# A hybrid recurrent decoder step on one core: compact diagonal blocks of inverses, and w_in read by groups of eight rows

## The chip, the cores and the metric

The kernel runs on one core of one Trainium2 chip, in float32. The metric is the device time of one launch in microseconds (us). TensorE, VectorE (DVE), ScalarE (ACT), GpSimd (POOL) and SyncE (SP) run side by side, each with its instructions in order; SP and ScalarE issue the DMAs, which 16 DMA engines carry out.

## The reference, cut to what matters

One layer: a normalised input is multiplied by w_in (1024 x 8208), and the columns of the product feed an RG-LRU branch, a gated-DeltaNet branch, their gates and two merge gates. In DeltaNet, each chunk of tokens needs the inverse of a unit lower-triangular matrix.

```python
u = rms_norm(x, norm_pre)
z = jnp.einsum('btd,de->bte', u, w_in)
...
decay = jnp.where(causal, jnp.exp(jnp.where(causal, diff, 0.0)), 0.0)
M = jnp.where(strict, jnp.einsum('nbhik,nbhjk->nbhij', kb, kc) * decay, 0.0)
P = -M
Tinv = jnp.broadcast_to(jnp.eye(C, dtype=M.dtype), M.shape)
for _ in range((C - 1).bit_length()):
    Tinv = Tinv + jnp.einsum('nbhij,nbhjk->nbhik', Tinv, P)
    P = jnp.einsum('nbhij,nbhjk->nbhik', P, P)
u = jnp.einsum('nbhij,nbhjv->nbhiv', Tinv, vc * bc[..., None])
...
merged = jax.nn.sigmoid(m_lru) * p_lru + jax.nn.sigmoid(m_gdn) * p_gdn
y = jnp.einsum('btd,de->bte', merged, w_out)
```

There are 2048 prompt tokens and 64 sample tokens, D_MODEL is 1024, and DeltaNet has 8 heads of 128 x 128.

## The kernel before, in words

The prompt is worked through in four blocks of 512 tokens (blkno 0 to 3); the 64 sample tokens ride along in block 0. x is loaded with tokens on the partitions, normalised (u_norm), transposed by TensorE in 32 (block 0: 40) pieces and split into a high and a low part (u_tile); each tile k of u holds 128 rows of the contraction. Every product with a weight is done three times (high x high, high x low, low x high: lines 551, 553, 555 in proj), in pieces of 128 output columns.

Weights. Their order is a list, worder. In block 0 each piece is loaded from its input (wload), split into two parts by ScalarE and VectorE (split, called in wfetch), and the pair whl is stored into a scratch tensor dW (wstore, line 279). Blocks 1 to 3 load whl from dW (line 300). whl has three buffers. In most of the first part of block 0 two pieces of w_in are loaded at once (raw, 256 columns, line 271), else one (raws, 128 columns, line 265); the loads put row k*128 + p of the weight on partition p, for k from 0 to 7.

DeltaNet runs in two phases per block. In the first, t_gram makes M for each head and chunk of 128 tokens and stores it in dM (line 780). When all 8 heads are done, t_inv loads the four 32 x 32 diagonal blocks of all 32 matrices as 128 small matrices, one per partition, and inverts them on VectorE (tri_inverse). The inverses and their transposes are stored into dD and dDT (lines 848 and 849), which hold full 128 x 128 matrices; their remaining parts have to be zero, and t_zero stores the zeros in block 0 (line 504). In the second phase, t_inv2 loads for each head M (Mt), the inverses (Dn) and their transposes (R) (lines 990 to 992), and a Neumann step on TensorE fills in the blocks of R off the diagonal; t_chain then runs over the chunks.

TensorE's order is fixed by a planner in the Python code, Weave: side tasks are generators that yield a time in ns or a condition, and proj lets it run one step of each due task after every product. The order of the other engines and of SP's queue is found by a scheduler at build time from the program order and its own estimates, so that it can change with any edit. A DMA on SP can also have to wait for the landing of an earlier one whose semaphore it takes over.

The lines that matter:

```python
SP.dma_start(raw, src[:, c:c + w].rearrange("(k p) c -> p k c", p=128))
...
tr(t[:, n:n + m], xt[:m, k * 128:(k + 1) * 128], ident[:m, :m])
...
SP.dma_start(dD[:, q, q], r[0][q])
SP.dma_start(dDT[:, q, q], r[1][q])
```

Of the kernel before, what the change touches and what calls it, by code (L numbers as in the profile page):

```python
# [154 lines left out]
def body(ctx, tc, x_prompt, x_sample, state_lru_conv, state_lru_h, state_gdn_conv, state_gdn_S,  # L155
# [28 lines left out]
    def gtile():  # L184
        t = pg.tile([128, 512], F32, name="g", tag="g")
        return t
# [8 lines left out]
    def tr(out, in_, idn):  # L195
        T.transpose(out, in_, idn)  # L196
        W.pe(TR)
# [41 lines left out]
    dW = [dram.tile([128, 2, 1024], F32, name=f"dW{i}") for i in range(len(wplace))]  # L239
    wstores, wraws = [], {}  # L240

    wready = []
    wlast = [None]
    wnext, lnext = [0], [0]
# [8 lines left out]
    def wload(n):  # L253

        src, c = e = worder[n]
        if key(e) in wraws:
            return
        if isinstance(c, tuple):
            raw = rw.tile([128, 4, 256], F32, name="rawo", tag="raws")
            SP.dma_start(raw, src[c[1] * 512:(c[1] + 1) * 512, c[0] * 256:(c[0] + 1) * 256]  # L260
                         .rearrange("(k p) c -> p k c", p=128))
            wraws[key(e)] = raw
        elif not (paired[0] <= n < paired[1] or paired[2] <= n < paired[3]):
            raw = rw.tile([128, 8, 128], F32, name="raws", tag="raws")
            SP.dma_start(raw, src[:, c:c + 128].rearrange("(k p) c -> p k c", p=128))
            wraws[key(e)] = raw
        else:
            two = [key(x) for x in worder[n:n + 7]].count((src.tensor.name, c + 128))
            w = 128 + 128 * two
            raw = rp[0].tile([128, 8, w], F32, name="raw", tag="raw")  # L270
            SP.dma_start(raw, src[:, c:c + w].rearrange("(k p) c -> p k c", p=128))
            for j in range(1 + two):
                wraws[src.tensor.name, c + 128 * j] = raw[:, :, 128 * j:128 * j + 128]

# [72 lines left out]
    def u_tile(xh, k):  # L347
        hi = pA.tile([128, TB + NS], F32R, name="a", tag="a")
        lo = pA.tile([128, TB + NS], F32R, name="a", tag="a")
        for gi, grp in enumerate([xh[:4]] + ([xh[4:]] if len(xh) > 4 else [])):  # L350
            t = gtile()
            n = 0
            for xt, m in grp:
                tr(t[:, n:n + m], xt[:m, k * 128:(k + 1) * 128], ident[:m, :m])
                n += m
            cs = slice(gi * 512, gi * 512 + n)
            act(hi[:, cs], t[:, :n], AF.Copy, scale=npre[:, k:k + 1])
            V.scalar_tensor_tensor(out=lo[:, cs], in0=t[:, :n], scalar=npre[:, k:k + 1],
                                   in1=hi[:, cs].bitcast(F32), op0=OP.mult, op1=OP.subtract)
        return hi, lo  # L360
# [23 lines left out]

    dk = dram.tile([H, 128, TB + NS], F32, name="dk")
    dM = dram.tile([H * NCH, 128, 128], F32, name="dM")
    dD = dram.tile([H * NCH, 128, 128], F32, name="dD")
    dDT = dram.tile([H * NCH, 128, 128], F32, name="dDT")
    dE = dram.tile([H, 128, TB], F32, name="dE")
    dtm = dram.tile([16, 128, TB + NS], F32, name="dtm")  # L390
    dgc = dram.tile([H * NCH, 128], F32, name="dgc")
# [19 lines left out]
    rows = lambda a: a.rearrange("o (g p) -> (o g) p", p=128)  # L411
    with tc.tile_pool(name="init", bufs=2, side="right") as ip:
        with tc.tile_pool(name="u0", bufs=1) as up:
            r0 = ip.tile([8, 128], F32, name="r0")
            SP.dma_start(r0, rows(norm_pre))
            xh = u_load(0, up)
            t = gtile()
            tr(t[:, :8], r0, ident[:8, :8])
            V.tensor_copy(npre, t[:, :8])
            wraw = ip.tile([128, 8, 16], F32, name="wraw", bufs=1)  # L420
            SP.dma_start(wraw, win[:, C_B:C_B + 16].rearrange("(k p) c -> p k c", p=128))
            u_norm(xh, up)
            for n in range(2):
                wload(n)
                lnext[0] += 1
            SP.dma_start(dtb, bass.AP(tensor=gdn_dt_bias.tensor, offset=gdn_dt_bias.offset, ap=[[0, 128], [1, 8]]))
            SP.dma_start(negA, bass.AP(tensor=gdn_A_log.tensor, offset=gdn_A_log.offset, ap=[[0, 128], [1, 8]]))
            u = [u_tile(xh, k) for k in range(8)]
            zz = ip.tile([128, 96], F32, name="zz", bufs=1)
            V.memset(zz, 0.0)  # L430
            V.tensor_copy(wst[:, 256:352], zz)
            V.tensor_copy(wst3[:, :, 0:16], wraw)
            V.tensor_tensor(out=wst3[:, :, 16:32], in0=wraw, in1=wst3[:, :, 0:16].bitcast(F32), op=OP.subtract)
            wfetch(2)
        G.affine_select(out=tri, in_=ones, pattern=[[1, 128]], compare_op=OP.is_ge, fill=0.0,
                        base=0, channel_multiplier=-1)
        G.affine_select(out=offm.rearrange("p (a b) -> p a b", b=32), in_=ones.rearrange("p (a b) -> p a b", b=32),
                        pattern=[[-32, 4], [0, 32]], compare_op=OP.is_ge, fill=0.0, base=-32,
                        channel_multiplier=1)
        V.tensor_scalar(offm, offm, -1.0, None, op0=OP.mult)  # L440

        blk = const.tile([64, 64], F32, name="blk")
        blk3 = blk.rearrange("p (a b) -> p a b", b=8)
        G.affine_select(out=blk3, in_=ones[:64, :64].rearrange("p (a b) -> p a b", b=8),
                        pattern=[[-8, 8], [0, 8]], compare_op=OP.is_ge, fill=0.0, base=0, channel_multiplier=1)
        G.affine_select(out=blk3, in_=blk3, pattern=[[8, 8], [0, 8]], compare_op=OP.is_ge, fill=0.0,
                        base=7, channel_multiplier=-1)
        tris = const.tile([64, 64], F32, name="tris")
        V.tensor_tensor(out=tris, in0=blk, in1=tri[:64, :64], op=OP.mult)
        negs = const.tile([64, 64], F32, name="negs")  # L450
        V.tensor_scalar(negs, tris, 1.0, BIG, op0=OP.subtract, op1=OP.mult)
        bsel = blk3[:, :, 0]
        G.memset(halog, 0.0)
        G.memset(halol, 0.0)
        G.memset(hlast, 0.0)
        tc.keep_in_program_order(A.activation(negA, negA, AF.Exp))
        V.tensor_scalar(negA, negA, -1.0, None, op0=OP.mult)
# [39 lines left out]
    def t_zero(pool):  # L497

        z = pool.tile([128, 4, 128], F32, name="lru7")
        G.memset(z, 0.0)  # L500
        for h in range(H):
            yield 7000.0
            for dst in (dD, dDT):
                SP.dma_start(dst[4 * h:4 * h + 4].rearrange("c i j -> i c j"), z)
        yield 7000.0
        SP.dma_start(dDs.rearrange("h i j -> i h j"),
                     z[:64].rearrange("p a b -> p (a b)").rearrange("p (a b) -> p a b", b=64))
        zeroed[0] = True
# [22 lines left out]
    for blkno in range(NBLK):  # L531
# [299 lines left out]
        def t_inv():  # L831
            yield lambda: all(kdone)
            Mb = kl.tile([128, 32, 32], F32, name="Mb", tag="Mbinv", bufs=1)
            for b in range(4):
                q = slice(32 * b, 32 * b + 32)
                SP.dma_start(Mb[q], dM[:, q, q])
            if sb:
                Mbs = kl.tile([64, 8, 8], F32, name="Mbs", tag="Mbinvs", bufs=1)
                for b in range(8):
                    q = slice(8 * b, 8 * b + 8)  # L840
                    SP.dma_start(Mbs[q], dMs[:, q, q])
            yield 3000.0
            r = []
            yield from tri_inverse(kl, 32, 128, Mb, "inv", r)
            yield lambda: zeroed[0]
            for b in range(4):
                q = slice(32 * b, 32 * b + 32)
                SP.dma_start(dD[:, q, q], r[0][q])
                SP.dma_start(dDT[:, q, q], r[1][q])
            yield T_IN  # L850
            invdone[0] = True
            if sb:
                r = []
                yield from tri_inverse(kl, 8, 64, Mbs, "invs", r)
                for b in range(8):
                    q = slice(8 * b, 8 * b + 8)
                    SP.dma_start(dDs[:, q, q], r[1][q])
# [121 lines left out]
        def h2t(nm, bufs=B2, shape=None):  # L979
            return h2.tile(shape or [128, NCH, 128], F32, name=nm, tag=nm, bufs=bufs)  # L980

        def t_inv2(h):

            d = st_[h]
            hc = slice(NCH * h, NCH * h + NCH)
            d["kT"] = h2t("kT", B2, [128, NB])
            SP.dma_start(d["kT"], dk[h, :, :NB])
            Mt, Dn = h2t("Mt", 1), h2t("Dn", 1)
            R = d["R"] = h2t("R")
            SP.dma_start(Mt, dM[hc].rearrange("c j i -> j c i"))  # L990
            SP.dma_start(Dn, dD[hc].rearrange("c j i -> j c i"))
            SP.dma_start(R, dDT[hc].rearrange("c j i -> j c i"))
            d["Ed"] = h2t("Ed")
            SP.dma_start(d["Ed"], dE[h].rearrange("p (c i) -> p c i", c=NCH))
            d["loaded"] = True
# [357 lines left out]
```

## Time and profile before

| what | value |
|---|---|
| median of 3 runs | 2675.2 us (2672.99 to 2676.81) |
| the profiled execution's own time | 2665.83 us |
| its span, first to last instruction | 2664.1 us |
| TensorE busy | 2564.3 us (96%) |
| VectorE, ScalarE, GpSimd busy | 1508.0, 886.9, 378.0 us |
| moved by DMA | 581.82 MB, mean 218 GB/s |

Busy time is the sum of an engine's instructions. A wait is told as the idle time of an engine before an instruction and what released it. The DMA share is the mean busy share of the 16 DMA engines; beside GB/s it tells whether transfers are many or slow. [...]

### The profile page before, as it was taken

How to read it: one execution, taken by the hardware profiler on the slowest of the kernel's cores; microseconds unless marked ns; L12 is line 12 of the kernel's file. 1: busy time of each engine (PE TensorE's matmuls, PEld its weight loads, DVE VectorE, ACT ScalarE, POOL GpSimd, SP SyncE). 2: the span in 40 equal slices, each digit the busy share in tenths (PEclk: the TensorE clock that was granted, in tenths of full speed). 3: DMA queues.
4: the chain of work that ended last, by engine and by line, in shares of the span. 5: the costliest groups of instructions: out<-in, count | busy, mean ns of one | idle time of the engine just before them, and what ended most of it. 6: DMA issues, size and time to landing. Idle time of an engine off the chain costs nothing.

```text
span 2664.1 us, 39927 instructions
## 1 busy us (share of the span) xinstructions
PE 2564.3 (96%) x15332; PEld 2232.2 (84%) x15332; DVE 1508.0 (57%) x3521; ACT 886.9 (33%) x1722; POOL 378.0 (14%) x364
## 2 busy tenths in 40 slices
PE   6988889998999999999999999999999999999999
PEld 5888888887999788888889888888889888888888
DVE  4668668776544457566513457566513457566512
ACT  5336533333333235333303235333303235333301
POOL 0220111001210111110200211110211211100210
PEclk9999999999999999999999999999999999999999
DMA  7997988788877786544466886644466886545465
GB/s 210 253 285 181 261 202 202 181 173 162 307 269 270 256 271 217 203 168 164 158 240 255 273 275 213 208 162 167 158 237 256 272 277 214 202 169 168 160 236 201
DMA packets 327897, 581.82 MB, mean 218 GB/s; under 512 B 70849, under 2 KB 236762, under 8 KB 282650
## 3 DMA queue, kind: packets, MB, share of 16 engines
q1 hardware_dynamic: 313882, 553.57, 66.6%
q10 hardware_dynamic: 13824, 25.70, 2.6%
q8 instruction: 121, 1.98, 0.3%
q14 instruction: 70, 0.57, 0.1%
HBM read 421.61 MB, written 157.59 MB: 217 GB/s over the span
## 4 chain that ended last, share of the span: by engine, by line
PE 77%; DMA 10%; DVE 6%; issue 2%; ACT 2%; SPq 1%; POOL 1%; ACTq 0%; POOLq 0%; DVEq 0%
PE mm L555 18%; PE mm L553 18%; PE mm L551 18%; PE g L192 8%; PE c L192 5%; PE g L196 2%; PE mm L1294 2%; PE mm L1296 2%; PE mm L1298 2%; DMA er<-dgc 2%; DMA raws<-in_w_in_dram 2%; DMA dW<-whl 2%; DVE cvy L582 1%; DVE whl L205 1%; DMA dE<-er 1%
## 5 line engine op out<-in xcount | busy, mean ns | idle before, releaser
L551 PE MATMUL mm<-a,whl 128*128 128x512 f32 (+2 forms) x2432 | 862.3, 355 | 15.6 <-ACT tmo L143 11.9
L555 PE MATMUL mm<-a,whl 128*128 128x512 f32 (+2 forms) x2432 | 867.4, 357 | 7.3 <-DVE whl L205 7.3
L553 PE MATMUL mm<-a,whl 128*128 128x512 f32 (+2 forms) x2432 | 862.1, 354 | 0.0
L551 PEld LDWEIGHTS mm<-a,whl 128*128 128x128 f32 x2432 | 464.7, 191 | 64.0 <-ACT tmo L143 12.7
L555 PEld LDWEIGHTS mm<-a,whl 128*128 128x128 f32 x2432 | 464.7, 191 | 60.8 <-DVE whl L205 8.3
L553 PEld LDWEIGHTS mm<-a,whl 128*128 128x128 f32 x2432 | 464.6, 191 | 45.5
L582 DVE SCALAR_TENSOR_TENSOR cvy<-cvr,cwg,cvy 128x512 f32<-128x512 f32 x288 | 217.4, 755 | 17.9 <-ACT cvy L143 12.5
L553 PE MATMUL mm<-a,whx 128*128 128x512 f32 x448 | 181.7, 406 | 0.0
L555 PE MATMUL mm<-a,whx 128*128 128x512 f32 x448 | 181.4, 405 | 0.0
L551 PE MATMUL mm<-a,whx 128*128 128x512 f32 x448 | 179.3, 400 | 0.0
L1232 DVE SCALAR_TENSOR_TENSOR pt<-tm,mm 128x512 f32<-128x512 f32 (+1 forms) x80 | 47.3, 592 | 180.7 <-PE mm L555 180.6
L143 ACT ACTIVATE cvr<-mm 128x512 f32<-128x512 f32 (+1 forms) x160 | 81.6, 510 | 186.9 <-PE mm L555 179.1
L1086 POOL TENSOR_TENSOR st<-st,mhalf 128x4 f32<-128x4 f32 x32 | 38.9, 1215 | 653.4 <-DVE st L1084 653.4
L1294 PE MATMUL mm<-whl,bt 128*128 128x256 f32 x448 | 126.2, 282 | 1.2 <-DVE y L1303 1.2
L1298 PE MATMUL mm<-whl,bt 128*128 128x256 f32 x448 | 126.2, 282 | 0.2 <-DVE yss L1272 0.2
L1296 PE MATMUL mm<-whl,bt 128*128 128x256 f32 x448 | 126.3, 282 | 0.0
L143 ACT ACTIVATE yv<-c 128x128 f32<-128x128 f32 x128 | 35.5, 277 | 245.9 <-PE c L192 245.4
L143 ACT ACTIVATE th<-cvy 128x512 f32<-128x512 f32 (+1 forms) x96 | 61.9, 645 | 156.4 <-DVE cvy L582 130.9
L555 PE MATMUL mm<-gp,whl 128*128 128x512 f32 (+2 forms) x296 | 104.2, 352 | 0.0
L551 PE MATMUL mm<-gp,whl 128*128 128x512 f32 (+2 forms) x296 | 104.1, 352 | 0.0
L553 PE MATMUL mm<-gp,whl 128*128 128x512 f32 (+2 forms) x296 | 104.0, 351 | 0.0
L551 PEld LDWEIGHTS mm<-a,whx 128*128 128x128 f32 x448 | 84.5, 189 | 17.6
(341 smaller groups left out, 4476.1 us busy)
## 6 DMA issues: line engine op xcount, KB each, us to landing
whl<-dW SPq DMA_DIRECT2D x199, 1024.0 KB
dW<-whl SPq DMA_DIRECT2D x88, 1024.0 KB
whx<-dW SPq DMA_DIRECT2D x65, 1024.0 KB
raws<-in_w_in_dram SPq DMA_DIRECT2D x33, 512.0 KB
raw<-in_w_in_dram SPq DMA_DIRECT2D x15, 1024.0 KB
dtm<-tmo ACTq DMA_DIRECT2D x48, 256.0 KB
tm<-dtm SPq DMA_DIRECT2D x48, 256.0 KB
ux<-in_x_prompt_dram SPq DMA_DIRECT2D x16, 512.0 KB
```

The lines of the kernel that those rows point to most:

```text
L143: r = f(*args, **kw)
L192: T.matmul(out, a, b, start=start, stop=stop)
L196: T.transpose(out, in_, idn)
L551: T.matmul(ps[:, :n], wh, mh[:, c0:c0 + n], start=k == 0, stop=False)
L553: T.matmul(ps[:, :n], wh, ml[:, c0:c0 + n], start=False, stop=False)
L555: T.matmul(ps[:, :n], lo[:, k, :], mh[:, c0:c0 + n], start=False, stop=k == 7)
L582: V.scalar_tensor_tensor(out=y[:, :TB], in0=raw[:, i:i + TB], scalar=cw[:, i, ti:ti + 1], in1=y[:, :TB], op0=OP.mult, op1=OP.add)
L1086: G.tensor_tensor(out=st[:, 3], in0=st[:, 2], in1=mhalf[:, :NCH], op=OP.pow)
L1232: proj(mov, lambda ps, c0, n: V.scalar_tensor_tensor(out=t_[:, c0:c0 + n], in0=x[:, c0:c0 + n], scalar=1.0, in1=ps[:, :n], op0=OP.add, op1 ...
L1294: T.matmul(ps[:, :256], mh[:, cs], wh[:, k % 4], start=k == 0, stop=False)
L1296: T.matmul(ps[:, :256], mh[:, cs], wl[:, k % 4], start=False, stop=False)
L1298: T.matmul(ps[:, :256], ml[:, cs], wh[:, k % 4], start=False, stop=k == 7)
```

## The change

Two changes that are independent of each other. First, dD and dDT hold only the diagonal blocks, [4, 32 matrices, 32, 32]: t_inv stores each with one DMA in one piece per partition, t_zero no longer stores zeros into them, and t_inv2 loads each head's blocks with four DMAs of 32 partitions into tiles blkd, which GpSimd clears once per block of tokens (two tiles that take turns for R, one for Dn). Second, krows puts rows 8p to 8p + 7 of w_in on partition p; u_tile takes every eighth column of x for the same order, and norm_pre is loaded straight into that order. The other weights keep theirs.

```diff
+    def krows(a, by8):
+
+        return a.rearrange("(p k) c -> p k c", k=8) if by8 else a.rearrange("(k p) c -> p k c", p=128)
+
...
-            SP.dma_start(raw, src[:, c:c + 128].rearrange("(k p) c -> p k c", p=128))
+            SP.dma_start(raw, krows(src[:, c:c + 128], src is win))
...
-            SP.dma_start(raw, src[:, c:c + w].rearrange("(k p) c -> p k c", p=128))
+            SP.dma_start(raw, krows(src[:, c:c + w], src is win))
...
-                tr(t[:, n:n + m], xt[:m, k * 128:(k + 1) * 128], ident[:m, :m])
+                tr(t[:, n:n + m], xt[:m].rearrange("t (p k) -> t k p", k=8)[:, k], ident[:m, :m])
...
-    dD = dram.tile([H * NCH, 128, 128], F32, name="dD")
-    dDT = dram.tile([H * NCH, 128, 128], F32, name="dDT")
+    dD = dram.tile([4, H * NCH, 32, 32], F32, name="dD")
+    dDT = dram.tile([4, H * NCH, 32, 32], F32, name="dDT")
...
-            r0 = ip.tile([8, 128], F32, name="r0")
-            SP.dma_start(r0, rows(norm_pre))
+            SP.dma_start(npre, norm_pre.rearrange("o (p k) -> (o p) k", k=8))
             xh = u_load(0, up)
-            t = gtile()
-            tr(t[:, :8], r0, ident[:8, :8])
-            V.tensor_copy(npre, t[:, :8])
             wraw = ip.tile([128, 8, 16], F32, name="wraw", bufs=1)
-            SP.dma_start(wraw, win[:, C_B:C_B + 16].rearrange("(k p) c -> p k c", p=128))
+            SP.dma_start(wraw, krows(win[:, C_B:C_B + 16], True))
...
-        G.memset(z, 0.0)
-        for h in range(H):
-            yield 7000.0
-            for dst in (dD, dDT):
-                SP.dma_start(dst[4 * h:4 * h + 4].rearrange("c i j -> i c j"), z)
+        G.memset(z[:64], 0.0)
         yield 7000.0
...
-            for b in range(4):
-                q = slice(32 * b, 32 * b + 32)
-                SP.dma_start(dD[:, q, q], r[0][q])
-                SP.dma_start(dDT[:, q, q], r[1][q])
+            for dst, m in ((dD, r[0]), (dDT, r[1])):
+                SP.dma_start(dst.rearrange("b n i j -> (b n) i j"), m)
...
+        blkd = []
+        for i in range(3):
+            blkd.append(h2.tile([128, NCH, 128], F32, name=f"blkd{i}"))
+            G.memset(blkd[i], 0.0)
+
...
-            Mt, Dn = h2t("Mt", 1), h2t("Dn", 1)
-            R = d["R"] = h2t("R")
+            Mt, Dn = h2t("Mt", 1), blkd[2]
+            R = d["R"] = blkd[h % 2]
             SP.dma_start(Mt, dM[hc].rearrange("c j i -> j c i"))
-            SP.dma_start(Dn, dD[hc].rearrange("c j i -> j c i"))
-            SP.dma_start(R, dDT[hc].rearrange("c j i -> j c i"))
+            for b in range(4):
+                q = slice(32 * b, 32 * b + 32)
+                SP.dma_start(Dn[q, :, q], dD[b, hc].rearrange("c i j -> i c j"))
+                SP.dma_start(R[q, :, q], dDT[b, hc].rearrange("c i j -> i c j"))
```

How this moves instructions is seen on SP's queue. The zeros first: SP in block 0, while head 0's M is being made, before the change (lru is the tile of zeros, dgc holds the gate sums that er reads back, dk takes the keys):

```order
L701 DMA dgc<-gr 32x128
L707 DMA dgs<-gr_813 8x64
L504 DMA dD<-lru_870 128x4x128
L504 DMA dDT<-lru_870 128x4x128
L504 DMA dD<-lru_870 128x4x128
L709 DMA ers<-dgs 64x512
L754 DMA er<-dgc 128x512
L807 DMA dk<-kT 128x576
```

The same place with the change:

```order
L697 DMA dgc<-gr 32x128
L703 DMA dgs<-gr_809 8x64
L269 DMA raws<-in_w_in_dram 128x8x128 x2
L705 DMA ers<-dgs 64x512
L750 DMA er<-dgc 128x512
L803 DMA dk<-kT 128x576
```

Three stores of zeros are gone from this place (the other 13 are gone from the places around it), and the scheduler has put two loads of 512 KB of w_in there, which stood some 250 us later before.

SP at the start of block 0's second phase, the loads of the first head (lines 990 to 992), before the change:

```order
L265 DMA raws<-in_w_in_dram 128x8x128
L987 DMA kT<-dk 128x576
L990 DMA Mt<-dM 128x4x128
L991 DMA Dn<-dD 128x4x128
L992 DMA R<-dDT 128x4x128
L994 DMA Ed<-dE 128x512
L265 DMA raws<-in_w_in_dram 128x8x128
```

And with the change (blkd_3911 is Dn, blkd_3907 is R):

```order
L269 DMA raws<-in_w_in_dram 128x8x128
L986 DMA kT<-dk 128x576
L989 DMA Mt<-dM 128x4x128
L992 DMA blkd_3911<-dD 32x4x32
L993 DMA blkd_3907<-dDT 32x4x32
L992 DMA blkd_3911<-dD 32x4x32
L993 DMA blkd_3907<-dDT 32x4x32
L992 DMA blkd_3911<-dD 32x4x32
L993 DMA blkd_3907<-dDT 32x4x32
L992 DMA blkd_3911<-dD 32x4x32
L993 DMA blkd_3907<-dDT 32x4x32
L995 DMA Ed<-dE 128x512
```

Two loads have become eight, alternating between the two tiles. TensorE's own order is the same but for the transpose of norm_pre.

## Rows read from the trace of the kernel before

**Rows 1.** Busy time by stage: stretch, length, then engines, PEclk, DMA share, GB/s.
```profile
0.00:40.00 40.00, 15.18 (x57) 10.71 (x58) 16.71 (x51) 19.29 (x33) 5.50 (x18) 1.00 0.67 147
40.00:370.00 330.00, 286.38 (x2011) 279.25 (x2011) 216.77 (x616) 153.41 (x293) 51.59 (x53) 0.94 0.89 241
...
600.00:680.00 80.00, 71.61 (x510) 64.08 (x509) 52.47 (x124) 24.35 (x55) 9.04 (x7) 0.96 0.85 174
...
860.00:1460.00 600.00, 594.06 (x3213) 497.29 (x3212) 316.72 (x711) 185.55 (x351) 86.67 (x82) 1.00 0.63 215
```

**Rows 2.** Waits of TensorE, 40 to 370 us: total us, times, longest.
```profile
PE g L192 <- ACT lt L143: 13.7, 3, 8.3
PE mm L551 <- ACT tmo L143: 11.9, 4, 5.5
PE mm L555 <- DVE whl L205: 7.3, 5, 2.8
PE g L192 <- DMA Dn<-dD: 6.8, 1, 6.8
```

**Rows 3.** Waits of ScalarE, 40 to 370 us.
```profile
ACT whl L143 <- DMA dW<-whl: 61.0, 14, 11.3
```

**Rows 4.** Busy time in four short stretches; the last two columns: DMA share, GB/s.
```profile
237.20:247.20 10.00, 9.04 (x62) 8.84 (x62) 10.00 (x29) 5.54 (x12) 1.83 (x3) 0.92 1.00 94
268.50:275.50 7.00, 6.16 (x47) 5.96 (x45) 4.69 (x17) 0.68 (x2) 0.96 (x2) 1.00 0.90 160
702.80:705.50 2.70, 2.70 (x22) 2.70 (x22) 0.11 (x1) 0.53 (x1) 0.00 (x0) 1.00 1.07 357
...
45.00:140.00 95.00, 85.21 (x624) 82.56 (x624) 54.41 (x181) 37.31 (x83) 16.80 (x18) 0.98 0.96 273
```

**Rows 5.** Timeline of SP's queue, 251 to 285 us: start, length, what.
```profile
252.53 0.43 SPq L271 DMA_DIRECT2D raw<-in_w_in_dram  x1
257.73 0.33 SPq L848 DMA_DIRECT2D dD<-invT  x1
...
273.15 0.74 SPq L849 DMA_DIRECT2D dDT<-invTT  x1
273.99 0.91 SPq L279 DMA_DIRECT2D dW<-whl  x1
```

**Rows 6.** Timeline of ScalarE, 265 to 290 us; in brackets the idle time before.
```profile
280.50 1.06 ACT L143 ACTIVATE whl<-raw 128x1024 fp32r<-128x1024 f32 x1 [11.32 <-DMA dW<-whl]
```

**Rows 7.** DMA issues by line: count, KB each.
```profile
raw<-in_w_in_dram SPq DMA_DIRECT2D x15, 1024.0 KB
...
dD<-lru SPq DMA_DIRECT2D x8, 256.0 KB
dDT<-lru SPq DMA_DIRECT2D x8, 256.0 KB
...
dD<-invT SPq DMA_DIRECT2D x16, 128.0 KB
```

**Rows 8.** TensorE's transposes of x (timeline); two VectorE groups: busy us, mean ns.
```profile
803.68 0.46 PEld L196 LDWEIGHTS g<-ident,ux 128*128 128x128 f32 x4
803.78 0.60 PE L196 MATMUL g<-ident,ux 128*128 128x128 f32 x4
...
L205 DVE TENSOR_TENSOR whl<-rawo,whl 128x1024 fp32r<-128x1024 f32 x8 | 9.8, 1225 | 6.4 <-ACT whl L143 6.4
...
L826 DVE COPY invTT<-invT 128x1024 f32<-128x1024 f32 x4 | 4.5, 1136 | 0.1
```

**Rows 9.** ScalarE's waits for raws, 0 to 40 and 600 to 680 us; a GpSimd clear.
```profile
ACT whl L143 <- DMA raws<-in_w_in_dram: 7.4, 3, 4.0
...
ACT whl L143 <- DMA raws<-in_w_in_dram: 6.8, 1, 6.8
...
L500 POOL MEMSET lru<- 128x512 f32 x1 | 0.5, 524 | 20.9 <-PE g L196 20.9
```

## The prediction

> **What bounds the kernel now.** Read the stages first [rows 1]. From 860 us on TensorE is busy 594.1 of 600 us at a granted clock of 1.00 in one block of tokens, and the two blocks behind it read alike: nothing that the change does to transfers can help there. Block 0 is another matter. From 40 to 370 us TensorE is busy 286.4 of 330 us, and its mean granted clock is 0.94 between the two levels of 1.2 and 2.4 GHz: 43.6 us idle and 330 x 0.06 = 19.8 us of lost clock, 63 us together. From 600 to 680 us another 8.4 + 3.2 us go. In the same stretches the DMA share is 0.89 and 0.85. So what can be won lies in block 0, where weights come from w_in.
>
> Next, who releases TensorE [rows 2]: ScalarE with lt (13.7 us) and tmo (11.9 us), VectorE with whl (7.3 us), the load of Dn (6.8 us). ScalarE itself waits 61.0 us in 14 waits for the *store* of an earlier weight, dW<-whl, before it may write the next whl [rows 3]; what stands behind it on ScalarE (lt, tmo, the emptying of PSUM) is late with it. Three whl buffers turn over, and a store that lands late stops ScalarE, then TensorE. So the bound of block 0 is the time that transfers need ahead of those stores.
>
> Last, how fast transfers go [rows 4]. From 237.2 to 247.2 us little but one load of w_in (1024 KB, 256 columns) is under way: the engines are busy all the time (1.00) and move 94 GB/s. The load of w_br from 702.8 to 705.5, in runs of the same 1 KB, gives 357 GB/s at 1.07. The difference is not run length. The rows of w_in that a partition takes lie 128 rows apart, and each row is 8208 columns long; w_br has 1024.
>
> **The change, term by term** (sum against the profiled execution's own 2665.8 us; the median of the runs shown, 2675.2, is 9.4 above, so I add that at the end). The full rate is 357 / 1.07 = 334 GB/s.
>
> *Zero stores.* Sixteen stores of 256 KB go (8 to dD, 8 to dDT [rows 7]), 4.2 MB or 12.6 us at 334 GB/s, all between 45 and 140 us, where the DMA share is 0.96 and TensorE loses 9.8 us of 95 [rows 4]. Bounds: 0, if the waits there come from w_in alone, to -10, all that TensorE loses. I take -5. Two loads of 512 KB of w_in now stand in the queue where three zero stores stood, ahead of head 0's er; they are moved, not added. At the worst rate they take 11 us, and head 0's matrix comes that much later; keys of three heads may stand unread, so TensorE goes on. Bounds 0 to +5, if ScalarE stops at head 0's er with the emptying of PSUM behind it; I take 0.
>
> *Stores of the inverses.* Before, eight stores of 128 KB in runs of 128 bytes stand on SP's queue from 257.73 to 273.9 us; the weight store behind them is issued only at 273.99 [rows 5]. ScalarE waits 11.32 us for it [rows 6], and TensorE 8.3 of its 13.7 us for lt [rows 2]. Now two stores, 512 KB each, in whole rows: 1.05 MB, 3.1 us. SP is free about 13 us earlier, but the load of w_in issued ahead of them at 252.53 still ends when it ends. Bounds 0 to -12 (8.3 and the low clock behind it); I take -8. The other blocks win nothing: TensorE doesn't wait there.
>
> *Loads of the diagonal blocks.* Two loads of 256 KB per head become eight of 16 KB. The runs shrink from 512 to 128 bytes and their number stays at 1024. Runs of 128 bytes moved at 160 GB/s and a share of 0.90 [rows 4], so a head's 128 KB cost about 0.7 us where 512 KB cost 1.6. Against that stand six more issues on SP, and for head 0 a first product that waits for the last of four pieces, with three of R's between. Bounds -7 (the wait of 6.8 us goes) to +5 (six issues in block 0's crowded queue, and large transfers behind them that wait for a small one's semaphore); I take 0. Three clears of 128 x 512 on GpSimd precede them per block, 0.5 us each [rows 9]; they end long before the loads unless GpSimd waits for old tiles, and blocks 1 to 3 hide it.
>
> *Rows of w_in.* Runs, bytes and issues stay; only the order of addresses changes: a partition takes eight neighbouring rows, and partitions stand 8 rows apart instead of one. Whether this cures the 94 GB/s, no row shows. Lower bound of the gain: below nothing (the slower rival). Upper: from 40 to 370 us 241 GB/s moved 79.5 MB, 238 us at 334 GB/s, while the engines were busy 0.89 x 330 = 294 us: 56 us of slowness. If all belong to the 15 loads of 1024 KB, each takes 3.1 + 3.7 = 6.8 us, against 11.2 at 94 GB/s. All cured, most of the 63 - 13 = 50 us, of the 11.6 us at 600 to 680 (ScalarE waits 6.8 us there for raws) and of the 7.4 us that it waits for raws in the first 40 us [rows 9] could go: -60. I take half the slowness cured and about a third of the losses: -15, -4 and -2, so -21. I lean to a gain because 1 KB runs at a step of 4 KB (w_br) are fast and those at jumps of 128 long rows are slow; neighbours lie nearer together, though still 32 KB apart.
>
> *Transposes of x.* Their weight loads now read every eighth element (32 bytes). Blocks 0 to 2 do 32 each in the output stage, where TensorE is busy throughout; four take 0.46 us, 0.115 each, under 0.60 us of products [rows 8]. No row shows TensorE reading with a step. The nearest: a VectorE copy that writes with a step of 128 bytes takes 1136 ns for 1024 elements, a contiguous operation 1225 [rows 8], no penalty. Bounds 0 to twice the time, 96 x 0.115 = +11, and up to +4.6 for the 40 at the start; I take +3, near the nearest row.
>
> *The gains' load.* norm_pre arrives directly as 128 x 8; one transpose and one copy go. It is needed only after the scaling of x: 0.
>
> Sum: -5 - 8 + 0 - 21 + 3 = -31, so 2634.8 profiled and **2644** as a median.
>
> **Rivals.**
> (a) *The row order leaves the rate as it is.* For it: the runs are the same 1 KB in rows 32 KB apart. Then -13 + 3: 2665.
> The Trainium skill (DMA: Bandwidth & Descriptors, Latency and other measured facts) gives rates that fall as the step between the rows of neighbouring partitions grows to large powers of two, from 512 KiB on. That step grows here from 32 KiB + 64 bytes to 256 KiB + 512, so by that rule nothing is won, and the time is (a)'s. The trace disagrees in part: 94 GB/s stands at the small step; (a) gets 0.12 for that and no more.
> (b) *Stepped weight reads take twice as long*: -31 - 3 + 15.6 = -18, 2657; with (a) as well, 2678, no change within what a measurement can tell (0.2%, 5.3 us). For it: nothing in the trace; against it: the VectorE copy [rows 8].
> The Trainium skill (SBUF — State Buffer, Door 1: The DMA port swizzle) says that accesses pay whenever they jump to a new 16-byte line, so that four float32 in a row are free; every element would pay here, and the time would be (b)'s. No run here shows it yet.
> (c) *Slower: the new order collides worse.* If the 15 loads all fall to the 94 GB/s of the worst, each costs 11.2 instead of 6.8 us: +66 us against 17 saved (12.6 and about 4). The engines' need rises from 294 to 343 us, over the stretch's 330, and at a share of 0.95 it lasts 361: +31, about 2706. It decides once a load takes over 6.8 + 17 / 15 = 7.9 us. For it: equal runs already differ from 94 to 357 GB/s by address alone. Against: 94 is nearly the worst shown.
> (d) *Nearly all slowness goes*: -13 - 50 + 3 = -60: 2615.
>
> **Chances.** Forecast 0.42 (its own range 2625 to 2662), (a) 0.12, (b) 0.13, (a) and (b) together 0.05, (c) 0.18, (d) 0.10. Range for 8 in 10: 2610, which takes in (d), to 2688, which takes in (a), (b) and the mild third of (c). Faster by over 0.2%: nearly all of the forecast and of (b), (d), and two thirds of (a), 0.69. Within 0.2%: the rest of these and most of (a) with (b), 0.11. Slower: (c) and what is left, 0.20.
>
> **What would show it.** Right: a load of w_in of 1024 KB in 3 to 5 us with the share at 1 and well over 150 GB/s; ScalarE's wait for dW<-whl from 40 to 370 us far under 61.0; no wait of 8 us for lt at 280; the blocks from 860 us on as long as before, within some 4 us for the transposes. Wrong: four weight loads of ux in over 0.8 us; a DMA share near 1.00 through block 0 at under 200 GB/s; GpSimd or SP holding the first loads of blkd back, with TensorE waiting at a head's first product in blocks 1 to 3.

## The result, and the profile after

The changed kernel took 2638.4 us (median of four runs, 2635.8 to 2639.6) against 2674.1 us before on the same chip: a ratio of 0.9868, 95% interval 0.9849 to 0.9887, so 36 us less. On a second chip (e5 below) the ratio was 0.9897 (0.9881 to 0.9912): 27 us less. Forecast: 2644 in 2610 to 2688.

Where did it come from? One operation of the heads (st<-st,mhalf, on GpSimd) runs 32 times, once for each head and block of tokens; its first start marks the end of what goes before block 0's heads, its last the end of the last block's. The view of one tile, of the kernel before:

```profile
L1086 POOL TENSOR_TENSOR st<-st,mhalf x32: 1006/1007/2534, 415.6 to 2515.9; 128x4 f32<-128x4 f32 x32
```

and of the changed kernel:

```profile
L1087 POOL TENSOR_TENSOR st<-st,mhalf x32: 1006/1007/1864, 388.2 to 2487.5; 128x4 f32<-128x4 f32 x32
```

The first starts 27.4 us earlier, the last 28.4; the spans of the two profiled executions differ by 28.4 too (2664.1 and 2635.7). Nearly all of it is won ahead of 390 us. The stages of the changed kernel (columns as in [rows 1]; PEclk, the third from the end, is TensorE's mean granted clock as a share of 2.4 GHz); the third stretch is moved by 27.4 us, so that it holds the work that [rows 1] shows at 600 to 680:

```profile
0.00:40.00 40.00, 15.09 (x56) 10.47 (x57) 16.75 (x50) 19.18 (x33) 5.49 (x18) 1.00 0.71 135
40.00:370.00 330.00, 303.01 (x2214) 295.14 (x2213) 232.38 (x666) 160.47 (x310) 49.31 (x57) 0.96 0.87 247
572.60:652.60 80.00, 75.13 (x540) 67.59 (x539) 54.95 (x128) 25.73 (x57) 11.47 (x9) 0.98 0.85 187
860.00:1460.00 600.00, 595.87 (x3230) 499.61 (x3229) 321.03 (x720) 185.97 (x355) 89.47 (x86) 1.00 0.61 210
```

From 40 to 370 us TensorE's idle time fell from 43.6 to 27.0 us, and the mean granted clock rose from 0.94 to 0.96 (330 x 0.02 = 6.6 us). The start won nothing. Around 600 us idle time fell from 8.4 to 4.9, but from the first head to the last the two kernels take 2100.3 and 2099.3 us: the rest gave it back.

ScalarE's waits from 40 to 370 us, against [rows 3]:

```profile
ACT er L143 <- POOL er L753: 39.7, 8, 7.3
ACT cvr L143 <- PE mm L551: 27.4, 13, 5.0
ACT whl L143 <- DMA dW<-whl: 11.0, 4, 6.8
```

The wait for the weight stores fell from 61.0 to 11.0 us; the other two, for er and cvr, were 30.4 us each before. TensorE's waits from 40 to 370 us, against [rows 2]:

```profile
PE g L192 <- DMA blkd<-dDT: 6.6, 1, 6.6
PE g L192 <- ACT lt L143: 6.0, 1, 6.0
PE g L192 <- DVE Mt L774: 4.9, 1, 4.9
PE mm L551 <- DVE whl L205: 4.5, 1, 4.5
PE mm L547 <- ACT tmo L143: 2.3, 1, 2.3
```

tmo went from 11.9 to 2.3, lt from 13.7 to 6.0. The wait for the diagonal blocks stayed, under another name (Dn 6.8, blkd 6.6). The wait for Mt, 4.9 us, is new.

### The profile page after: what moved, and what is told of

Same layout as the page of the kernel before. It is cut to its first block, busy times and chain, and to the rows that moved or that the text cites. A ratio compares the mean times of both kernels' runs of the same rounds, so it can differ in the third digit from the quotient of the medians.

```text
span 2635.7 us, 40218 instructions
## 1 busy us (share of the span) xinstructions
PE 2556.1 (97%) x15331; PEld 2225.4 (84%) x15331; DVE 1504.0 (57%) x3520; ACT 885.9 (34%) x1722; POOL 380.4 (14%) x376
## 4 chain that ended last, share of the span: by engine, by line
PE 79%; DMA 9%; DVE 6%; ACT 2%; POOL 1%; issue 1%; SPq 1%; ACTq 0%; POOLq 0%; DVEq 0%
PE mm L551 19%; PE mm L549 19%; PE mm L547 19%; PE g L192 8%; PE c L192 5%; PE g L196 2%; PE mm L1295 2%; PE mm L1299 2%; PE mm L1297 2%; DMA raws<-in_w_in_dram 2%; DMA er<-dgc 2%; DVE cvy L578 1%; DMA dW<-whl 1%; DVE whl L205 1%; DMA ers<-dgs 1%
## 5 line engine op out<-in xcount | busy, mean ns | idle before, releaser
L192 PEld LDWEIGHTS g<-blkd,Mt 128*32 128x32 f32 (+1 forms) x1024 | 78.0, 132 | 44.0 <-issue 30.1
L192 PE MATMUL g<-blkd,Mt 128*128 128x128 f32 (+3 forms) x1024 | 96.4, 238 | 9.2 <-DMA blkd<-dDT 7.5
L551 PE MATMUL mm<-gp,whl 128*128 128x512 f32 (+2 forms) x296 | 104.2, 352 | 0.0
L547 PE MATMUL mm<-gp,whl 128*128 128x512 f32 (+2 forms) x296 | 104.1, 352 | 0.0
```

The lines of the kernel that those rows point to most:

```text
L192: T.matmul(out, a, b, start=start, stop=stop)
L547: T.matmul(ps[:, :n], wh, mh[:, c0:c0 + n], start=k == 0, stop=False)
L551: T.matmul(ps[:, :n], lo[:, k, :], mh[:, c0:c0 + n], start=False, stop=k == 7)
```

## The experiments

Runs of one kernel spread by 2 to 14 us, and chips differ (before took 2666.5 to 2674.1), so differences go by ratios or by medians of the same chip; medians of two chips are a rough guide only. "dW" is ScalarE's wait for the weight stores from 40 to 370 us.

| run | median us | before there | ratio (95%) | zero stores | dW us |
|---|---|---|---|---|---|
| e1 compact blocks alone | 2647.3 | 2670.2 | 0.9918 (0.9906-0.9929) | none | 11.7 |
| e2 rows alone | 2658.4 | 2670.2 | 0.9962 (0.9949-0.9976) | 16 | 47.0 |
| e3 zero stores back | 2649.2 | 2670.2 | 0.9925 (0.9913-0.9936) | 16 | 41.8 |
| e4 short stores back | 2643.0 | 2670.2 | 0.9899 (0.9886-0.9911) | none | 7.4 |
| e5 the changed kernel again | 2639.0 | 2666.5 | 0.9897 (0.9881-0.9912) | none | 9.0 |
| e6 zero stores of a quarter | 2647.6 | 2666.5 | 0.9926 (0.9910-0.9941) | 16 x 64 KB | 28.7 |
| e7 plain transposes | 2640.6 | 2666.5 | 0.9895 (0.9877-0.9912) | none | 10.2 |
| e8 two queues for head 0 | 2647.2 | 2666.5 | 0.9922 (0.9907-0.9936) | none | 8.6 |
| e11 loads not ahead | 2633.8 | 2668.8 | 0.9875 (0.9862-0.9887) | none | 9.6 |
| e12 before, loads ahead | 2671.4 | 2668.8 | 1.0013 (1.0004-1.0023) | 16 | 62.6 |
| e13 zero stores, loads ahead | 2652.0 | 2668.8 | 0.9943 (0.9929-0.9957) | 16 | 47.9 |
| e14 columns shifted | 2642.4 | 2668.8 | 0.9904 (0.9890-0.9917) | none | 9.9 |

The first four runs weigh two theories: S, that the zero stores and the short stores of the inverses held the weight stores back, and R, that the order of w_in's rows did.

**e1, the compact blocks alone** (against the changed kernel; norm_pre as before too).

```diff
-            SP.dma_start(raw, krows(src[:, c:c + w], src is win))
+            SP.dma_start(raw, krows(src[:, c:c + w], False))
...
-                tr(t[:, n:n + m], xt[:m].rearrange("t (p k) -> t k p", k=8)[:, k], ident[:m, :m])
+                tr(t[:, n:n + m], xt[:m, k * 128:(k + 1) * 128], ident[:m, :m])
```

> The compact diagonal blocks alone; w_in's rows, the transposes of x and norm_pre as before. Theory S (the stores theory): what held ScalarE back 61.0 us in 14 waits for dW<-whl was mostly the zero stores and the sixteen-descriptor-short stores of the inverses standing in front of the weight stores; then this part alone gives at least two thirds of the 36 us: 24 to 34 us faster than before, and the waits for dW from 40 to 370 us fall under 25 us. Theory R (the rows theory): the order of w_in's rows gives most; then this part alone gives 0 to 10 us, and the waits for dW stay at 45 us or more. The sum of the prediction (zeros -5, inverse stores -8, loads 0): 13 us faster.

**e2, the rows alone**: the kernel before with krows(..., src is win), the stepped transposes and the direct load of norm_pre, nothing else.

> The eight neighbouring rows per partition alone, with the stepped transposes of x and the direct load of norm_pre; zero stores, stores and loads of the diagonal blocks as before. Theory S: 0 to 10 us faster than before, waits of ScalarE for dW from 40 to 370 us at 40 us or more. Theory R: 24 to 34 us faster, and those waits under 25 us. The sum of the prediction (rows -21, transposes +3): 18 us faster. If the stepped transposes were dear (0.115 us each for 96), it would be slower than Theory R by 11 us.

e1 is 22.9 us faster than before, e2 11.8 (by the ratios 21.9 and 10.1), and together 34.7: within the spread the two halves add up to the whole change. dW falls to 11.7 us in e1 and only to 47.0 in e2; in e1 and then in e2:

```profile
ACT whl L143 <- DMA dW<-whl: 11.7, 3, 7.6
```

```profile
ACT whl L143 <- DMA dW<-whl: 47.0, 12, 10.3
```

Theory S has two thirds, just under the 24 to 34 us that it expected; R is out as the main cause, but the rows are worth as much as S allows at most, or a little more. By what the rows win it, no run shows.

**e3, the zero stores back**, into dZ, which nobody reads.

```diff
...
-        G.memset(z[:64], 0.0)
+        G.memset(z, 0.0)
+        for h in range(H):
+            yield 7000.0
+            for dst in dZ:
+                SP.dma_start(dst[4 * h:4 * h + 4].rearrange("c i j -> i c j"), z)
```

> The changed kernel with the sixteen zero stores of 256 KB put back where they stood, into buffers that nobody reads. The prediction's term: 5 us slower than the changed kernel, bounds 0 to 10. Theory S: 10 us or more slower, TensorE between 45 and 140 us loses more than now, and ScalarE waits again for dW. Theory R: within 3 us of the changed kernel.

10 us more than the changed kernel by medians (7 to 15 by the ratios to either measurement of it), and dW is back at 41.8 us: as S says.

**e4, the short stores back**, eight DMAs in runs of 128 bytes into rows padded to 64 numbers.

```diff
-            for dst, m in ((dD, r[0]), (dDT, r[1])):
-                SP.dma_start(dst.rearrange("b n i j -> (b n) i j"), m)
+            for b in range(4):
+                q = slice(32 * b, 32 * b + 32)
+                SP.dma_start(dD[b, :, :, :32], r[0][q])
+                SP.dma_start(dDT[b, :, :, :32], r[1][q])
...
```

> The changed kernel with the inverses stored by eight DMAs in runs of 128 bytes, as before, into a compact buffer whose rows are padded to 64 numbers; no zero stores; loads of the diagonal blocks as changed. The prediction's term: 8 us slower than the changed kernel, bounds 0 to 12, with a wait of ScalarE for dW of about 11 us at 270 to 280 us and of TensorE for lt behind it. If the wait at 280 us came from the load of w_in ahead (that at 252 us) and not from these stores, the difference stays under 2 us.

0 to 8 us more: by the ratios, 0.9899 against 0.9897 and 0.9868 for the two measurements of the changed kernel; by medians 4 (2643.0 to 2639.0). SP stands at the eight stores for 12.7 us, before for 16.3 [rows 5]; in the timeline of e4 (SPq is SP's queue):

```profile
248.97 0.65 SPq L844 DMA_DIRECT2D dD<-invT  x1
250.12 1.18 SPq L845 DMA_DIRECT2D dDT<-invTT  x1
251.35 5.22 SPq L844 DMA_DIRECT2D dD<-invT  x1
...
259.93 1.68 SPq L845 DMA_DIRECT2D dDT<-invTT  x1
261.65 1.82 SPq L283 DMA_DIRECT2D dW<-whl  x2
```

but the next whl on ScalarE that is late at all starts after 0.47 us, and not for a store:

```profile
274.19 1.06 ACT L143 ACTIVATE whl<-raw 128x1024 fp32r<-128x1024 f32 x1 [0.47 <-ACT tmo L143]
```

So these stores alone do not make a wait like the 11.32 us of [rows 6]. Where the zero stores stand, a wait of that kind is there with either form, in e2 with the old stores and in e3 with the new ones:

```profile
270.88 1.06 ACT L143 ACTIVATE whl<-raw 128x1024 fp32r<-128x1024 f32 x1 [10.32 <-DMA dW<-whl]
```

```profile
258.69 1.06 ACT L143 ACTIVATE whl<-raw 128x1024 fp32r<-128x1024 f32 x1 [7.67 <-DMA dW<-whl]
```

This part of theory S falls as the reason of that wait. But the old form is not free beside the zero stores: e2 and e3 ran on the same chip and differ in the stores and loads of the diagonal blocks and in the buffers that the zeros go to, and e3 is 9.2 us faster (10 by the ratios). Which of these it is, no run shows.

**e5, the changed kernel again**, as base for e6 to e8.

> The changed kernel itself once more, as the base for the runs beside it. 2638.4 us, within 4 us.

**e6, zero stores of a quarter**: as e3, with `dst[4 * h:4 * h + 4, :32]` and `z[:32]`.

> The changed kernel with sixteen zero stores at the old places, but of 64 KB each (32 of the 128 partitions): the same number of issues and steps, a quarter of the bytes, into buffers that nobody reads. With the full stores back the kernel took 2649.2 us, 11 us more than the changed kernel did. If their bytes cost the time (4.2 MB, 12.6 us of all sixteen queues at the full rate), a quarter of that is left: 2 to 4 us slower than the changed kernel, and ScalarE's waits for dW stay under 25 us. If their issue and their steps in the order of the work cost it, it is 9 us or more slower.

8.5 us slower than e5 on the same chip (2 to 14 by the two intervals), just under what was expected if issues and steps cost it; dW is over the 25 us that the bytes would allow:

```profile
ACT whl L143 <- DMA dW<-whl: 28.7, 9, 8.8
```

That is much of the cost of e3 at a quarter of its bytes. So the bytes, on which both my term and my reading of e3 rested, are hardly the main cost of the zero stores; e11 below makes this firmer.

**e7, plain transposes**: `xt[:m, k * 128:(k + 1) * 128]` in the changed kernel.

> The changed kernel with the transposes of x reading 128 neighbouring columns as before, while w_in's rows stay in the new order; so the contraction pairs wrong rows, and nothing else differs. The prediction's term is 3 us for the stepped reads: then this is 3 us faster than the changed kernel, with weight loads of ux at 158 ns again instead of 198. The trace of the changed kernel (four weight loads 0.53 instead of 0.46 us) gives 0.02 us each, under 2 us in all: then this is within 2 us of the changed kernel. If every element read paid a line of its own, it would be 10 us or more faster.

1.5 us slower than e5, within the spread. The weight loads of x in the changed kernel (min, median, max in ns):

```profile
L196 PEld LDWEIGHTS g<-ident,ux x136: 182/193/231, 7.7 to 2005.5; 128*128 128x128 f32 x128, 64*128 64x128 f32 x8
L196 PE MATMUL g<-ident,ux x136: 274/277/479, 7.7 to 2005.6; 128*128 128x128 f32 x128, 64*128 64x64 f32 x8
```

and in e7:

```profile
L196 PEld LDWEIGHTS g<-ident,ux x136: 137/142/231, 8.2 to 2010.6; 128*128 128x128 f32 x128, 64*128 64x128 f32 x8
L196 PE MATMUL g<-ident,ux x136: 270/273/476, 8.2 to 2010.7; 128*128 128x128 f32 x128, 64*128 64x64 f32 x8
```

The step does cost 51 ns a load, but a load stays shorter than its product (277 ns), beside which it runs.

**e8, two queues for head 0.**

```diff
-            for b in range(4):
-                q = slice(32 * b, 32 * b + 32)
-                SP.dma_start(Dn[q, :, q], dD[b, hc].rearrange("c i j -> i c j"))
-                SP.dma_start(R[q, :, q], dDT[b, hc].rearrange("c i j -> i c j"))
+            for dst, src in ((Dn, dD), (R, dDT)):
+                for b in range(4):
+                    q = slice(32 * b, 32 * b + 32)
+                    Q = G if h == 0 and dst is R else SP
+                    Q.dma_start(dst[q, :, q], src[b, hc].rearrange("c i j -> i c j"))
```

> The changed kernel with all four pieces of Dn issued ahead of those of R, and head 0's pieces of R issued from GpSimd instead of SP. TensorE waits 6.6 us at 330 to 336 us for the pieces that SP issues between 325.7 and 335.0. If that wait is the interleaved issue on SP, it falls by 3 us or more, and the kernel is 2 to 5 us faster than the changed kernel; if it is the time that SP comes to these loads at all (it stood at a load of w_in until 322.6) or the landing of Mt and kT, the wait stays and the time is within 2 us.

The first product of head 0 in the changed kernel, and then in e8, by TensorE's timeline:

```profile
336.17 2.04 PE L192 MATMUL g<-blkd,Mt 128*128 128x128 f32 x8 [6.56 <-DMA blkd<-dDT]
```

```profile
336.63 2.05 PE L192 MATMUL g<-blkd,Mt 128*128 128x128 f32 x8 [5.87 <-DMA blkd<-dD]
```

The wait stays, although the last piece goes out at 331 us instead of 335: SP comes to head 0's loads only at 323 us (324 in e8). The kernel is 8 us slower than e5, which neither expectation had; where that comes from was not followed up. The profiled runs are nearly equal (2643.2 and 2643.1 us of span), but e5's was the slowest of its five and e8's the second fastest. A single difference of 8 us between two kernels, such as e6's, therefore proves little by itself.

After e6, two theories were left. O: the zero stores cost by what they displace, namely two loads of 512 KB of w_in, which every kernel without zero stores so far issues at some 66 us and every kernel with them at some 280 us or later. B: the stores themselves, by issues or by their steps in the order of the work.

**e11, the changed kernel with these loads held back.**

```diff
...
+            if n in (35, 36):
+                tc.add_manual_dep(r.ins, slast[0].ins.name,
+                                  mybir.DependencyInfo(mybir.DependencyClass.NoSync, mybir.DependencyReason.DATA),
+                                  reason="not ahead")
```

> The changed kernel (no zero stores) with the two loads of 512 KB of w_in that it issues at 66 us held to about their old place, behind the stores of the weights 31 and 32. Theory O (order): the zero stores cost little by their bytes; what they did was to keep these two loads at some 280 us, behind free buffers and in the crowded queue. Then this is 6 to 11 us slower than the changed kernel (about 2646 to 2650 us), like the kernel with a quarter of the zero bytes, and ScalarE's waits for dW from 40 to 370 us rise over 20 us. Theory B (the stores themselves, by bytes, issues or steps): within 3 us of the changed kernel.

**e12, the kernel before with these loads ahead**, and **e13, e3 with them ahead**: in both, behind the store to dgs,

```diff
+                if blkno == 0:
+                    wload(35)
+                    wload(36)
```

> The kernel before, whole, with nothing but these two loads issued early (behind dgs, before 66 us) instead of at some 280 us. Theory O: 6 to 14 us faster than before, with the zero stores still there. Theory B: within 4 us of before, or slower, since 1 MB more stands in the queue while the zero stores fill it.

> The changed kernel with all sixteen zero stores of 256 KB back, and the two loads issued early all the same. Theory O: within 4 us of the changed kernel, against 11 us more with the stores back and the loads late. Theory B: 9 us or more above the changed kernel. In between, bytes and order share it.

O falls three times over. e11 loses nothing: its four runs (2632.7 to 2635.7) all lie below the nine of the changed kernel, though on another chip, and by the ratios it is level with it. e12 is 2.6 us slower than before. e13 pays 13 us against e5 by medians, with dW at 47.9.

The two loads cost something when they go early, rather than win. Every kernel that issues them early has a wait of TensorE for head 0's Mt near 90 us, 3.4 to 5.5 us long (4.9 in the changed kernel, 9.4 in e14); the five that issue them late (before, e2, e3, e6, e11) have none. So the zero stores are best priced between kernels that treat these loads alike, by the ratios: e3 and e6 against e11 13 and 14 us (0.9925 and 0.9926 to 0.9875), e13 against the changed kernel 12 or 20 (0.9943 to 0.9897 or 0.9868). In the traces the first head (st<-st,mhalf) starts 10.1 and 12.1 us later in e3 and e6 than in e11. Within the spread a quarter of the bytes costs as much as all of them.

What the traces show instead of O is the spacing of the loads of 1024 KB (raw) on SP. In the changed kernel, from 95 to 165 us:

```profile
102.29 1.44 SPq L275 DMA_DIRECT2D raw<-in_w_in_dram  x1
...
117.49 0.60 SPq L275 DMA_DIRECT2D raw<-in_w_in_dram  x1
...
132.74 0.74 SPq L275 DMA_DIRECT2D raw<-in_w_in_dram  x1
...
148.56 0.60 SPq L275 DMA_DIRECT2D raw<-in_w_in_dram  x1
...
161.26 1.34 SPq L275 DMA_DIRECT2D raw<-in_w_in_dram  x1
```

In e6, with the small zero stores:

```profile
101.26 0.79 SPq L275 DMA_DIRECT2D raw<-in_w_in_dram  x1
...
114.49 0.60 SPq L275 DMA_DIRECT2D raw<-in_w_in_dram  x1
...
142.89 0.61 SPq L275 DMA_DIRECT2D raw<-in_w_in_dram  x1
...
147.46 0.77 SPq L275 DMA_DIRECT2D raw<-in_w_in_dram  x1
```

In the changed kernel a load goes out every 13 to 16 us. In e6 none goes out for 28 us, then two within 5; so it is wherever the zero stores stand: 117.72, 150.89, 156.18 in the kernel before, 113.16, 141.62, 146.65 in e3, 124.72, 150.23, 158.06 in e13. The weight stores behind such a pair are late, and ScalarE with them (7.87 us at 154.4 in e6). The changed kernel has one such pair, later (178.51, 202.72, 204.73), and its longest wait for dW, 6.80 us up to 225.9, stands behind it. But not all of it lies behind the pair: in e6 ScalarE waits 4.72 us for a store already up to 129.9 us, inside the gap, and in the kernel before 10.00 us up to 137.9, so the late load can also be an effect of the wait. All six kernels with zero stores show 28.7 us of dW or more, all others 11.7 or less; TensorE's waits for tmo from 40 to 370 us are 10.5 to 16.1 us in the six, 4.6 or less in the others. That the zero stores bring these waits is shown; that the spacing is the way was only read from these rows. No run kept the even spacing with the stores in place, so whether their issues or the order they force costs the 12 to 14 us stays open.

**e14, the columns shifted.**

```diff
-            SP.dma_start(raw, krows(src[:, c:c + w], src is win))
+            c2 = c if src is not win else c - 256 if c else 256
+            SP.dma_start(raw, krows(src[:, c2:c2 + w], src is win))
```

> The changed kernel with every load of w_in of 1024 KB taken 256 columns (1 KB) lower, the first pair of the LRU columns 1 KB higher, so that the products use other columns; sizes, issues and order stay. In the trace of the changed kernel the slow loads of 1024 KB are three of fifteen (the stretches 230 to 240 us at 127 GB/s and two like it), and they are those whose runs start 3072 to 3136 bytes above a multiple of 4096. If that place sets the rate, the slow ones are now the second and the fourteenth of the fifteen, and the stretches around 120, 230 and 245 us run at over 150 GB/s; the time changes by a few us, less waiting around 225 to 245 us. If it is what else is under way then, the slow stretches stay where they are.

The three slow loads of the changed kernel, numbers 5, 12 and 13 of the fifteen (last two columns: DMA share and GB/s, all traffic):

```profile
106.00:116.00 10.00, 10.00 (x78) 9.80 (x77) 7.59 (x23) 4.20 (x8) 0.54 (x1) 1.00 1.01 149
212.50:222.50 10.00, 8.91 (x66) 8.62 (x64) 10.00 (x22) 5.75 (x9) 1.31 (x3) 1.00 1.03 136
231.50:241.50 10.00, 5.51 (x42) 5.30 (x40) 9.80 (x33) 4.38 (x9) 1.76 (x1) 0.97 1.00 114
```

In e14, number 2 of the fifteen, then the same three places in the order, then number 14:

```profile
46.00:56.00 10.00, 10.00 (x78) 10.00 (x78) 6.55 (x32) 7.65 (x17) 0.00 (x0) 1.00 1.03 161
110.00:117.00 7.00, 7.00 (x53) 6.80 (x53) 6.40 (x23) 3.46 (x8) 0.54 (x1) 1.00 0.97 233
212.00:218.00 6.00, 6.00 (x47) 6.00 (x46) 6.00 (x18) 5.57 (x7) 1.02 (x1) 1.00 1.04 281
232.50:237.50 5.00, 5.00 (x32) 5.00 (x31) 5.00 (x20) 0.38 (x1) 0.00 (x0) 0.83 0.95 224
260.00:270.00 10.00, 10.00 (x79) 10.00 (x78) 7.84 (x18) 6.25 (x13) 0.91 (x1) 1.00 0.97 113
```

The slow loads moved with the columns. The whole time did not change (ratio 0.9904, e5 0.9897), with two slow loads for three. One of the two now stands ahead of head 0's keys, and TensorE's wait for Mt is 9.4 us, in e5 5.1; that the one makes the other was not tried.

## Why the prediction was right, and where it was not

The time, 2638 us, lies 6 us from the forecast and in its own narrower range. The bound was read rightly: block 0, and in it the weight stores that ScalarE waits for [rows 3]; from 860 us on nothing moved. But most of the terms were off, in both directions, so that the sum fits as well as it does is in part luck.

- **Zero stores, -5 (0 to -10).** Mis-sized, beyond the bound: 12 to 14 us, by one comparison 20, where the two loads are treated alike (7 to 15 by e3 against the changed kernel). And the reason given, 4.2 MB at 334 GB/s, failed: within the spread a quarter of the bytes costs as much (e6). I priced the stores as traffic and never asked what sixteen more entries do to the other transfers on SP's queue.
- **The two loads ahead, 0 (0 to +5).** Within the bounds, but not nothing: I held that TensorE goes on because keys of three heads may stand unread, and it waits 4.9 us for head 0's Mt in the changed kernel, not at all where the loads are late (e11). In time they cost 2.6 us in e12, 5 in e13 against e3 by the ratios, and between -2 and +6 in the changed kernel against e11.
- **Stores of the inverses, -8 (0 to -12).** The reason failed: I gave the 11.32 us of [rows 6] to the stores that stand ahead of the weight store in [rows 5]. With those stores back in the changed kernel, that wait does not come back (e4); with the zero stores back and these not, one of 7.67 us does (e3). The size is open: 0 to 8 us by e4 without the zero stores, and about 9 beside them, together with the loads of the diagonal blocks (e2 against e3).
- **Loads of the diagonal blocks, 0 (-7 to +5).** No run measures this term alone. The wait did not go: Dn's 6.8 us became 6.6 for the last of the pieces. The pieces' issues are not its cause, since it stays when half of them leave SP (5.9 us in e8).
- **Rows of w_in, -21, and transposes, +3.** Mis-sized: the two together give 10 to 12 us in e2, and e7 shows no cost of the transposes. I took half of the slowness as cured; but the slow loads that I had measured at 94 GB/s [rows 4] are set by their columns, which the change leaves (e14). By what the rows still win 10 to 12 us stays open. Of the places where I booked it, the start won none of its 2 us, and the 4 us around 600 us were given back by the last head.
- **Sum.** -13 for the compact half, measured 22.9; -18 for the other, measured 11.8; -31, measured 27 to 36.

The rivals. (a), that the row order leaves the rate as it is: its time is out, by the interval of e2; whether the rate rose, no run shows, and the three slow loads stayed slow. The row pitch of the Trainium skill (DMA: Bandwidth & Descriptors, Latency and other measured facts), by which nothing would be won, does not give the outcome here: 10 to 12 us were won. (b), stepped weight reads at twice the time: out; 193 ns stand against 142, a third more, beside products of 277. That the reads pay when they jump to a new 16-byte line, as the Trainium skill (SBUF — State Buffer, Door 1: The DMA port swizzle) says, agrees with the trace, but they do not take twice as long, and the time does not show it. The VectorE copy in [rows 8], which showed no penalty, was no guide to TensorE's reads. (c), worse collisions: out; three of fifteen loads are slow, as before, not all. (d), nearly all slowness gone: no, as the same three show.

## What to carry to other kernels

A transfer in a queue that one engine issues in order can cost more than its bytes, and a small one as much as a large one: remove or shrink one and look at when its neighbours are issued before pricing its bytes. A wait behind a row of stores is not yet those stores' wait; put them back alone to see, and also beside what else was there, since the answer can differ. When a change moves other transfers as well, compare kernels in which those stand alike. When two halves of a change are mis-sized in opposite directions the sum looks right, so run each half by itself.

## What the runs showed of the hardware

- A load of 1024 KB of w_in (runs of 1 KB in rows of 32 KB + 64 bytes) runs slow or fast by the place of its columns: with runs that start 3072 to 3136 bytes above a multiple of 4096 in the first row, the stretches above moved 113 to 161 GB/s with the queues full, at other columns 224 to 281. Both orders of the rows keep this: in the kernel before, the ten us from 107.5, 237.2 and 255 us on, in which the same three loads run, moved 130, 94 and 119 GB/s. Why that place is slow is open, since every load's runs pass through all places as the rows go on by 64 bytes.
- Weight loads of 128 x 128 float32 with a step of 32 bytes took 193 ns, against 142 in a row; beside products of 277 ns that did not show in the time (e7).
- Sixteen stores of 64 KB on SP's queue cost as much, within the spread, as sixteen of 256 KB: 14 and 13 us by the ratios (e6 and e3 against e11).
